# Moving the weights and the stationary tiles of a hybrid SSM and attention block to one SBUF address residue

## The chip, the cores and the metric

The kernel runs on one NeuronCore of one Trainium2 chip. The metric is the device time of one execution in microseconds (us), compared between kernels on the same chip. TensorE (PE) multiplies matrices: a weight load (PEld) puts the *stationary* operand into the array, and a matmul streams the *moving* operand past it. VectorE is DVE, ScalarE is ACT, GpSimd is POOL, and SyncE (SP) issues most DMAs. A tile of SBUF, the working memory, has 128 partitions, and its address is the byte at which it begins in each partition. "Residue" below is this address modulo 512.

## The reference

One layer over 2048 tokens of width 1024, all in float32:

```python
hn = rmsnorm(h, mix_norm_g[i])
proj = hn @ w_in[i]
u, g_ssm, q, k, v, g_attn = jnp.split(proj, SPLITS, axis=-1)
y_ssm = s5_branch(u, ...) * jax.nn.silu(g_ssm)           # diagonal complex SSM, GELU, GLU
y_att = stick_breaking_branch(q, k, v, q_norm_g[i], k_norm_g[i]) * jax.nn.silu(g_attn)
h = h + jnp.concatenate([y_ssm, y_att], axis=-1) @ w_out[i]
ple_gate = jax.nn.sigmoid(rmsnorm(h, ple_norm_g[i]) @ w_ple_gate[i])
h = h + ple_gate * (p[i] @ w_ple_proj[i])
```

The two 1024 x 1024 products at the end, with `w_out` and with `w_ple_gate`, are what the change is nearest to.

## The kernel before

**Split products.** A float32 product is made of three float32r products: each operand is split into a high part and the rest, and high x high, high x low and low x high are added up in PSUM. `mm3` (lines 541 to 543) does this with the weights as stationary operand, `mm3x` (lines 707 to 709) with the activations as stationary and 512 columns of weights as moving operand. `split` makes the parts: ACT copies the high part (line 513), DVE subtracts it (`vt`, line 65).

**Stages.** `phase_u` projects the SSM input (`ps_u`); SSM batches alternate with gate units (`ps_sg`) and the first attention projections (`ps_qk`); then come 40 steps of attention, in which four pairs of heads follow each other with a lag of 8 steps (projections `ps_q` on two halves of the rows, line 745; scores `ps_z`, line 812; transposes `ps_wt`, line 526; output `ps_o`, line 843). The GLU of the SSM branch (`ps_g2` and `ps_v2`, which the profile shows as `ps_g` and `ps_v` on `zr`) runs among the last ten steps.

**The output stage** is `phase_out`. For each of eight pairs of token tiles `mixed_pair` multiplies with `w_out` (`ps_h`), and then for each pair `gated_pair` multiplies with `w_ple_gate` (`ps_g` on `yr`) and with `w_pp` (`ps_p` on `pr`). Both use `cross_products`: a 2 x 2 block product with seven instead of eight block multiplications. For each of the seven, POOL or DVE forms a sum `sx` of blocks (line 912), `split` makes `yr` of it, and `mm3x` runs on four chunks of 128: 12 matmuls of 128 rows, 128 stationary and 512 moving columns. The weights of products 0 to 3 are in tiles `w` of the pool `w`, those of product 4 in halves of `xt` tiles (`wx`), those of products 5 and 6 in `wc` tiles of the pool `w3`. `gated_pair` first transposes `h` four times (`ps_t`, line 999).

In `mixed_pair` the callback `early` runs after product 2 and after product 3; `late` runs for each of the four output blocks and has ACT sum the squares of a block into a corner of `ss` (line 977).

**Where tiles lie.** Pools stand in two stacks: the left one grows up from byte 16512, the right one down from 229344. Within a pool the tags follow each other in the order of their first `tile()` call, and a slot takes a multiple of 32 bytes. At the bottom of the left stack is `const` (`warm` first, then `ident` and eight small tiles), above it `w` (16 weight tiles of 4096 bytes), `stage`, then `gx` and later `xp`, and at the end `fin`, which holds `yq`, `ss0`, `yr`, `sx`, `r`, `u` and small sums in this order. On the right are `kv0`, `proj`, `kv1`, `attn`, and at the end `w3` and `hr`, with `wc`, `wp`, `pr` and `h`. Keys and values are in `kv0`, `kv1` (right) and `kv2` (left), by the table `KV_SLOT`.

**Order.** `plan` collects what each instruction depends on, the bytes that a tile shares with older tiles included, `list_schedule` and `best_order` order every engine's instructions by estimated durations in six turns forward and back, and `arrange` writes that order down as dependences. An engine executes its own list in order; SP's list holds nearly all DMAs.

Of the kernel before, what the change touches and what calls it, by code (L numbers as in the profile page):

```python
# [8 lines left out]
F32 = mybir.dt.float32  # L9
# [3 lines left out]
AF = mybir.ActivationFunctionType  # L13
ALU = mybir.AluOpType
# [4 lines left out]
P = 128  # L19
# [44 lines left out]
def vt(nc, out, a, b, op):  # L64
    nc.vector.tensor_tensor(out, a, b, op=op)  # L65


def vs(nc, out, a, s1, op0, s2=None, op1=None):
    if op1 is None:
        nc.vector.tensor_scalar(out, a, s1, None, op0=op0)  # L70
    else:
        nc.vector.tensor_scalar(out, a, s1, s2, op0=op0, op1=op1)  # L72
# [830 lines left out]
def cross_products(e, pool, name, q, w, early, late, eng=None):  # L903

    nc = e.nc

    def f(tag, n):
        return pool.tile([P, 512], F32, tag=tag, name=tag, bufs=n)

    def add(a, b, op=ALU.add):  # L910
        t = f("sx", 3)
        (eng or nc.gpsimd).tensor_tensor(t, a, b, op=op)  # L912
        return t

    def product(ps, a, k, first):
        y = pool.tile([P, 2, 4, P], F32R, tag="yr", name="yr", bufs=4)
        split(e, y[:, 0].rearrange("p c t -> p (c t)"), y[:, 1].rearrange("p c t -> p (c t)"), a)
        for c in range(4):
            mm3x(e, ps, (y[:, 0, c], y[:, 1, c]), (w[k][c][:, 0], w[k][c][:, 1]), first and c == 0, c == 3, not first)

    ps = [e.bank(name, "z0", "z1", "acc", "ssm", "w0", *(("w1",) if name == "ps_h" else ())) for _ in range(4)]
    product(ps[0], q[0], 0, True)
    s1 = add(q[2], q[3])
    s2 = add(s1, q[0], ALU.subtract)
    r = f("r", 1)
    nc.scalar.activation(r, ps[0], AF.Copy)
    product(ps[1], s2, 1, True)
    u = f("u", 2)
    vt(nc, u, ps[1], r, ALU.add)
    product(ps[2], s1, 2, True)  # L930
    early(u, ps[2], 0)
    s3 = add(q[0], q[2], ALU.subtract)
    product(ps[3], s3, 3, True)
    early(u, ps[3], 1)
    product(ps[0], q[1], 4, False)
    late(0, ps[0], None)
    late(3, None, None)
    s4 = add(q[1], s2, ALU.subtract)
    product(ps[2], s4, 5, False)
    late(1, ps[2], u)  # L940
    product(ps[3], q[3], 6, False)
    late(2, ps[3], u)


def mixed_pair(e, pool, far, j):

    nc = e.nc
    dma = (nc.sync if j else nc.gpsimd).dma_start
    q, h = [], []
    for k in range(4):  # L950
        i = 2 * j + k // 2
        y = pool.tile([P, 512], F32, tag="yq", name="yq", bufs=5)
        v = y.rearrange("p (c t) -> p c t", c=4)
        if k % 2:
            dma(v, e.ya_d[i].rearrange("c p t -> p c t"))
        else:
            dma(v, e.ys_d[i // 4][:, (i % 4) * P:(i % 4 + 1) * P].rearrange("(c p) t -> p c t", p=P))
        q.append(y)
    for k in range(4):
        i = 2 * j + k // 2  # L960
        x = far.tile([P, 512], F32, tag="h", name="h", bufs=7)
        dma(x, e.x[0, i * P:(i + 1) * P, 512 * (k % 2):512 * (k % 2) + 512])
        h.append(x)
    ss = pool.tile([P, 2, 2], F32, tag=f"ss{j}", name="ss")

    def early(u, ps, n):
        if n == 0:
            for k in (3, 1, 2):
                nc.gpsimd.tensor_tensor(h[k], h[k], u, op=ALU.add)
        vt(nc, h[3], ps, h[3], ALU.add)  # L970

    def late(k, ps, u):
        if ps is not None:
            vt(nc, h[k], ps, h[k], ALU.add)
        i, m = k // 2, k % 2
        jk = far.tile([P, 512], F32, tag="sg", name="jk", bufs=4)
        nc.scalar.activation(jk, h[k], AF.Square, accum_out=ss[:, i, m:m + 1])
        nc.sync.dma_start(e.h_d[2 * j + i][:, 512 * m:512 * m + 512], h[k])

    cross_products(e, pool, "ps_h", q, e.wo, early, late, nc.vector if j < 2 else None)  # L980
    r = pool.tile([P, 2], F32, tag=f"rs{j}", name="rs")
    vt(nc, r, ss[:, :, 0], ss[:, :, 1], ALU.add)
    vs(nc, r, r, 1.0 / DM, ALU.mult, EPS, ALU.add)
    nc.gpsimd.tensor_tensor(r, r, e.mhalf[:, :2], op=ALU.pow)
    return r
# [51 lines left out]
def phase_out(e, pool, far, wpool2, wo4):  # L1037
    e.wo += [wo4] + [cross_weights(e, e.w_out[0], e.so_d, None, p, tag="wc", pool=wpool2, bufs=8) for p in range(5, 7)]
    rs = []
    for j in range(NT // 2):  # L1040
        rs.append(mixed_pair(e, pool, far, j))
        if j == 1:
            e.wp = [load_w(e, row_blocks(e.w_pp[0], 2, 512 * k), 512, None, tag="wp", pool=wpool2, bufs=4) for k in range(2)]
    e.wg = [cross_weights(e, e.w_pg[0], e.sg_d, e.gple, p, **(dict(pool=Halves(e)) if p == 4 else dict(tag="wc", pool=wpool2, bufs=8) if p > 4 else {})) for p in range(7)]
    for j in range(NT // 2):
        gated_pair(e, pool, far, j, rs[j])
# [3 lines left out]
def hybrid_block_kernel(ctx: ExitStack, tc: tile.TileContext, x, xt, small, p, w_in, ssm_w_glu, w_out, w_ple_gate,  # L1050
                        w_ple_proj, out, rows, pools, dbg=None):
    nc = tc.nc
# [25 lines left out]
    def const(name, shape, dt=F32):  # L1078
        return cp.tile(shape, dt, tag=name, name=name)

    warm = const("warm", [P, 1])
    nc.vector.memset(warm, 0.0)
    nc.scalar.activation(warm, warm, AF.Sigmoid)
    e.ident = const("ident", [P, P])
# [142 lines left out]
    for t in range(steps):  # L1227
# [7 lines left out]
        for hp in range(NHP):  # L1235
            i = t - SKEW * hp
# [385 lines left out]
```

## Time and profile before

| what | value |
|---|---|
| three runs | 1482.73, 1484.56, 1485.21 us; median 1484.56 us |
| span of the profiled execution, first to last instruction | 1479.9 us (the page gives that execution's time only as this span) |
| mean granted TensorE clock | 0.995 |
| PE busy | 1442.7 us, 97% of the span |
| weight loads busy, beside PE | 1222.7 us, 83% |
| DVE, ACT, POOL busy | 1010.3, 809.6, 473.1 us |
| DMA | 238.21 MB, mean 161 GB/s |

The runs' time also holds what lies before the first and after the last instruction. In the windows of the profile the columns are the stretch, its length, then busy time and number of instructions of each engine that has some (PE, PEld, DVE, ACT, POOL), the granted clock, the share of the DMA engines, and GB/s. In the timeline they are start and duration in us, engine, line, operation, out<-in (for a matmul, moving then stationary operand), and what the engine waited for. The duration of a matmul is modelled, and matmuls overlap; their starts are what can be compared. In the groups by tile the three numbers are the shortest, the median and the longest duration in ns.

### The profile page before, as it was taken

To read this page: it belongs to the slowest core of one execution; us is meant where nothing else is said; L and a number is where in the kernel's file an instruction comes from. 1 tells how busy PE (TensorE), PEld (TensorE's weight loads), DVE (VectorE), ACT (ScalarE), POOL (GpSimd) and SP (SyncE) were. 2 spreads that over 40 slices of the span, in tenths; PEclk is the share of its full clock that TensorE was granted. 3 is DMA by queue.
4 is the path that set the end of the run, shared out by engine and by line. 5 is a ranking of instruction groups with operands and counts; after the bars stand their busy time and mean duration, and the time that the engine had idled before them with its cause. 6 is when DMAs were issued, how large, how long until landed. Compare 5 with 4: busy or idle time off the path is not lost.

```text
span 1479.9 us, 33585 instructions
## 1 busy us (share of the span) xinstructions
PE 1442.7 (97%) x13068; PEld 1222.7 (83%) x13068; DVE 1010.3 (68%) x1817; ACT 809.6 (55%) x1765; POOL 473.1 (32%) x512
## 2 busy tenths in 40 slices
PE   6999999999999999999999999999999999999998
PEld 5999889988888888888888877787777887777776
DVE  8953877977567886678766766665787557844444
ACT  5654555655555766566655755465655435533332
POOL 3121364422221212121122115443234554433432
PEclk9999999999999999999999999999999999999999
DMA  8886846644333433334333455766477546423221
GB/s 289 286 285 208 247 140 192 198 155 154 136 134 114 149 116 115 107 123 143 116 129 126 125 133 188 237 204 185 137 245 244 182 156 209 143 71 100 86 74 55
DMA packets 179054, 238.21 MB, mean 161 GB/s; under 512 B 65760, under 2 KB 121296, under 8 KB 167760
## 3 DMA queue, kind: packets, MB, share of 16 engines
q1 hardware_dynamic: 176512, 227.49, 47.5%
q0 software_dynamic: 2384, 8.59, 2.0%
q8 instruction: 103, 1.69, 0.5%
q14 instruction: 55, 0.45, 0.1%
HBM read 166.94 MB, written 64.90 MB: 157 GB/s over the span
## 4 chain that ended last, share of the span: by engine, by line
PE 79%; DVE 9%; issue 3%; ACT 3%; POOL 3%; DMA 2%; SPq 0%; POOLq 0%; DVEq 0%; ACTq 0%
PE ps_q L745 21%; PE ps_o L843 8%; PE ps_z L812 6%; PE ps_wt L526 4%; PE ps_g L707 4%; PE ps_h L707 3%; PE ps_h L709 3%; PE ps_h L708 3%; PE ps_g L709 3%; PE ps_g L708 3%; DMA v<-qn 2%; PE ps_u L541 1%; PE ps_u L543 1%; PE ps_u L542 1%; POOL sx L912 1%
## 5 line engine op out<-in xcount | busy, mean ns | idle before, releaser
L821 DVE TENSOR_TENSOR_SCAN px<-px,ps_z 128x512 f32<-128x512 f32 (+3 forms) x320 | 339.9, 1085 | 84.8 <-ACT px L816 61.5
L745 PE MATMUL ps_q<-w_w,xt 64*128 64x512 f32 x2784 | 375.6, 398 | 1.3 <-DVE qn L65 0.7
L745 PEld LDWEIGHTS ps_q<-w_w,xt 64*128 64x128 f32 x2784 | 269.7, 185 | 39.9 <-DVE qn L65 2.0
L816 ACT ACTIVATE px<-ps_z 128x512 f32<-128x512 f32 (+3 forms) x320 | 159.2, 536 | 80.8 <-PE ps_z L812 79.5
L835 ACT ACTIVATE ws<-ps_wt 128x512 f32<-128x512 f32 (+3 forms) x320 | 160.8, 539 | 72.0 <-PE ps_wt L526 67.1
L812 PE MATMUL ps_z<-k,q 64*128 64x512 f32 (+3 forms) x960 | 137.8, 379 | 3.6 <-DVE px L821 1.8
L843 PE MATMUL ps_o<-ws,v 128*64 128x128 f32 x2176 | 135.2, 276 | 0.0
L843 PEld LDWEIGHTS ps_o<-ws,v 128*64 128x64 f32 x2176 | 117.6, 137 | 17.8 <-issue 14.9
L507 POOL TENSOR_TENSOR rs_qk<-rs_qk,mhalf 128x4 f32<-128x4 f32 x64 | 67.6, 1057 | 155.0 <-DVE rs_qk L72 152.4
L526 PEld LDWEIGHTS ps_wt<-ident,px 64*128 64x128 f32 x2176 | 95.5, 138 | 24.6 <-issue 5.5
L812 PEld LDWEIGHTS ps_z<-k,q 64*128 64x128 f32 x960 | 87.9, 186 | 21.6 <-issue 5.6
L526 PE MATMUL ps_wt<-ident,px 64*128 64x64 f32 x2176 | 101.0, 224 | 1.9 <-ACT ws L835 1.8
L819 POOL TENSOR_SCALAR_AFFINE_SELECT px<-px 128x128 f32<-128x128 f32 x128 | 40.6, 327 | 166.5 <-ACT px L816 157.3
L756 POOL TENSOR_TENSOR v<-qn,v 128x128 f32<-128x128 f32 x64 | 32.2, 504 | 161.4 <-DMA v<-qn 146.9
L541 PE MATMUL ps_u<-xt,w_w 128*128 128x256 f32 x256 | 75.5, 296 | 8.2 <-ACT w_w L491 6.9
L65 DVE TENSOR_TENSOR yr<-sx,yr 128x512 fp32r<-128x512 f32 x64 | 50.7, 814 | 42.0 <-ACT yr L513 41.2
L543 PE MATMUL ps_u<-xt,w_w 128*128 128x256 f32 x256 | 74.1, 296 | 2.0 <-DVE w_w L76 2.0
L542 PE MATMUL ps_u<-xt,w_w 128*128 128x256 f32 x256 | 74.9, 294 | 0.5 <-DVE xt L65 0.5
L1031 POOL TENSOR_TENSOR sg<-sg,h 128x512 f32<-128x512 f32 x28 | 39.6, 1414 | 95.6 <-DVE sg L65 94.2
L513 ACT ACTIVATE yr<-sx 128x512 fp32r<-128x512 f32 x64 | 39.1, 627 | 55.5 <-POOL sx L912 25.8
L65 DVE TENSOR_TENSOR qn<-ps_q,part 128x512 f32<-128x512 f32 x54 | 36.8, 681 | 42.7 <-ACT part L751 39.1
L513 ACT ACTIVATE yr<-yq 128x512 fp32r<-128x512 f32 x48 | 30.3, 631 | 55.4 <-PE ps_h L709 23.3
(438 smaller groups left out, 3492.3 us busy)
## 6 DMA issues: line engine op xcount, KB each, us to landing
xt<-hn SPq DMA_DIRECT2D x58, 1024.0 KB
hn<-xt SPq DMA_DIRECT2D x16, 1024.0 KB
h<-h SPq DMA_DIRECT2D x64, 256.0 KB
wst<-in_w_in_dram SPq DMA_DIRECT2D x48, 256.0 KB
xg<-hn SPq DMA_DIRECT2D x12, 1024.0 KB
out_dram<-sg SPq DMA_DIRECT2D x31, 256.0 KB
x<-in_x_dram SPq DMA_DIRECT2D x14, 512.0 KB
h<-in_x_dram SPq DMA_DIRECT2D x28, 256.0 KB
```

The source lines that it names most:

```text
L526: e.nc.tensor.transpose(ps[h][:, 64 * k:64 * k + 64], v[r], e.ident[r, r])
L541: mm(out, wh, xh, start=first, stop=False)
L542: mm(out, wh, xl, start=False, stop=False)
L543: mm(out, wl, xh, start=False, stop=last)
L707: mm(out, xh, wh, start=first, stop=False, skip_group_check=more)
L708: mm(out, xh, wl, start=False, stop=False, skip_group_check=more)
L745: nc.tensor.matmul(o, xt[r, a, c], A.w[c][r, b], start=c + s == 0, stop=c == NC8 - 1 and s == 2)
L812: nc.tensor.matmul(z[:, :n], q[half[h], a], A.k[ch][half[h], b, :n], start=s == 0, stop=s == 2)
L816: nc.scalar.activation(px[:, :n], z[:, :n], AF.Sigmoid, scale=-(HD ** -0.5))
L821: nc.vector.tensor_tensor_scan(rv, rv, z[:, :n][:, ::-1], initial=1.0 if carry[h] is None else carry[h], op0=ALU.mult, op1=ALU.bypass)
L835: nc.scalar.activation(dst, ps, AF.Copy, bias=1.0, scale=-1.0)
L843: nc.tensor.matmul(po[half[h], :P], A.v[sb][:, h], w[:, h, b], start=sb == i, stop=sb == 0)
```

## The change

Two allocations change; every instruction keeps its operands. The constant `warm`, of which one column is used, gets 24 columns. In `mixed_pair` the tile of the sums of squares, `ss`, is allocated when `early` first runs, after `yr`, `sx`, `r` and `u`, instead of at the start of the pair, between `yq` and `yr`. As each pair has its own tag `ss0` to `ss7`, only `ss0` stood before `yr`.

```diff
-    ss = pool.tile([P, 2, 2], F32, tag=f"ss{j}", name="ss")
+    sums = []
 
     def early(u, ps, n):
         if n == 0:
+            sums.append(pool.tile([P, 2, 2], F32, tag=f"ss{j}", name="ss"))
             for k in (3, 1, 2):
                 nc.gpsimd.tensor_tensor(h[k], h[k], u, op=ALU.add)
         vt(nc, h[3], ps, h[3], ALU.add)
...
-        nc.scalar.activation(jk, h[k], AF.Square, accum_out=ss[:, i, m:m + 1])
+        nc.scalar.activation(jk, h[k], AF.Square, accum_out=sums[0][:, i, m:m + 1])
...
-    vt(nc, r, ss[:, :, 0], ss[:, :, 1], ALU.add)
+    vt(nc, r, sums[0][:, :, 0], sums[0][:, :, 1], ALU.add)
...
-    warm = const("warm", [P, 1])
+    warm = const("warm", [P, 24])[:, :1]
```

## The prediction

> **What bounds the kernel now.** I read the page's first two parts, then the chain of work that ended last, then windows, waits and timeline of the last quarter, where the tiles lie that change their place against each other.
>
> ```profile
> span 1479.9 us, 33585 instructions
> PE 1442.7 (97%) x13068; PEld 1222.7 (83%) x13068; DVE 1010.3 (68%) x1817; ACT 809.6 (55%) x1765; POOL 473.1 (32%) x512
> PEclk9999999999999999999999999999999999999999
> PE 79%; DVE 9%; issue 3%; ACT 3%; POOL 3%; DMA 2%; SPq 0%; POOLq 0%; DVEq 0%; ACTq 0%
> ```
>
> TensorE is busy 97% of the span, at full clock, and holds 79% of the chain. An average says little about one stage, so here is the output stage (`ps_h` and `ps_g`, the only stage that reads `yr`), by windows and by PE's waits in it; the last window row counts the instructions on `yr` alone (PE, PEld, DVE, ACT).
>
> ```profile
> 1093.00:1253.00 160.00, 160.00 (x726) 128.25 (x723) 107.18 (x156) 75.70 (x157) 79.87 (x59) 1.00 0.64 206
> 1253.00:1281.00 28.00, 26.56 (x123) 20.76 (x122) 25.60 (x33) 18.65 (x34) 10.27 (x7) 1.00 0.58 185
> 1281.00:1475.00 194.00, 192.25 (x869) 151.98 (x867) 92.81 (x125) 71.49 (x119) 74.26 (x54) 1.00 0.25 80
> ...
> PE ps_g L707 <- ACT yr L513: 2.7, 6, 1.2
> PE ps_t L999 <- ACT yq L1001: 0.2, 1, 0.2
> ...
> 1093.00:1475.00 382.00, 325.28 (x1344) 248.50 (x1344) 96.83 (x112) 67.96 (x111) 1.00 0.44 141
> ```
>
> PE is busy 378.8 of these 382 us and waits 2.9 us in all: a matmul that takes less is time off the end. 1344 matmuls use `yr` as stationary operand. The mean duration of a matmul is modelled and pipelined, so I take the distance between starts. One unbroken run of `ps_h`, first and last row, with its window row (541 matmuls):
>
> ```profile
> 1125.44 0.40 PE L707 MATMUL ps_h<-w_w,yr 128*128 128x512 f32 x1
> ...
> 1251.44 0.39 PE L709 MATMUL ps_h<-w_wc,yr 128*128 128x512 f32 x1
> ...
> 1125.44:1251.44 126.00, 126.00 (x541) 101.25 (x540) 38.72 (x45) 26.44 (x42) 1.00 0.58 188
> ```
>
> 126.00 us over 540 steps is **233.3 ns** a matmul. Now the same form of matmul (128 rows, 128 columns, 512 moving columns, three per block as in the split product) on other tiles: `ps_p` inside this stage, `ps_v` of the GLU, `ps_qk` of the first projections.
>
> ```profile
> 1369.51 0.39 PE L707 MATMUL ps_p<-w_wp,pr 128*128 128x512 f32 x1
> ...
> 1372.25 0.27 PE L999 MATMUL ps_t<-ident,h 128*128 128x128 f32 x1
> ...
> 1079.05 0.39 PE L541 MATMUL ps_v<-zr,w_w 128*128 128x512 f32 x1
> ...
> 1081.55 0.39 PE L543 MATMUL ps_v<-zr,w_w 128*128 128x512 f32 x1
> ...
> 195.51 0.40 PE L708 MATMUL ps_qk<-w_w,xg 128*128 128x512 f32 x1
> ...
> 200.51 0.39 PE L709 MATMUL ps_qk<-w_w,xg 128*128 128x512 f32 x1
> ...
> 1341.85 0.39 PE L707 MATMUL ps_p<-w_wp,pr 128*128 128x512 f32 x1
> ...
> 1344.39 0.39 PE L709 MATMUL ps_p<-w_wp,pr 128*128 128x512 f32 x1
> ```
>
> Twelve `ps_p` take 2.74 us (228.3 ns each); `ps_v` takes 2.50 us for 11 steps (227.3), `ps_qk` 5.00 us for 22 (227.3); the slowest unbroken run of `ps_p`, the last two rows, takes 2.54 us for 11 (230.9). So a `yr` product costs some 5 ns more than these, in the same stage too.
>
> **The change part by part.** First the addresses. The left pools start at 16512, a slot takes a multiple of 32 bytes: `warm` 32, `ident` 512 and eight small constants of 32 put the weights at 17312, which is 416 modulo 512. All that follows up to `fin` is a multiple of 512, so `w`, `xg`, `xt`, `zr` are all at 416. In `fin` come five `yq` (10240 bytes), then `ss0` (32 bytes), so `yr` starts at **448**. The right pools go down from 229344 (480): `wc`, `wp`, `pr` are at 480. So today `ps_qk`, `ps_v` (416 with 416) and `ps_p` (480 with 480) have both operands at one residue, and only the `yr` products do not: 448 with 416 (five of seven products of a pair) or with 480 (two).
>
> *`warm` of 24 columns.* Its slot grows from 32 to 96 bytes, so every left tile moves up by 64: weights, `xt`, `zr` to 480. The instructions on it still take one column: cost 0, with nothing needed to hide it.
>
> *`ss` allocated in `early`.* No instruction or DMA is issued by an allocation, none passes another queue. Its slot now follows `yr`, `sx`, `r`, `u`, so `yr` moves by 64 - 32: 448 to 480, the residue of `w`, `wx`, `wc`. `sums[0]` is made before its first use in `late`; no wait is added.
>
> *The price of a `yr` matmul afterwards.* No `yr` product at equal residues is in this trace, so I bound it by the rows above: 227.3 at best, 230.9 at worst; 228.0 is taken, nearest to `ps_p` of the same stage, which has the same neighbours. Could the 5 ns come from other engines' traffic instead? This stretch has DVE, ACT and POOL all idle (window row, then first and last matmul on `yr` in it):
>
> ```profile
> 1305.70:1308.10 2.40, 2.40 (x12) 1.94 (x11) 0.00 (x0) 0.00 (x0) 0.00 (x0) 1.00 0.50 155
> ...
> 1305.62 0.40 PE L709 MATMUL ps_g<-w_wc,yr 128*128 128x512 f32 x1
> ...
> 1307.72 0.40 PE L709 MATMUL ps_g<-w_wc,yr 128*128 128x512 f32 x1
> ```
>
> Nine steps in 2.10 us: 233.3 with nothing else running. Traffic isn't it, nor the moving operand, since `w_w` at 416 and `w_wc` at 480 give the same. What is left to tell the groups apart is where `yr` lies. PEld is busy 101.25 of the 126.00 us in which PE streams, so both operands are read at once, and a clash that depends on their addresses is possible. 1344 x (233.3 - 228.0) = **7.1 us**; with the bounds 3.2 us (230.9) to 8.1 us (227.3).
>
> The Trainium skill speaks against this: the page "SBUF — State Buffer", section "Who interferes with whom", gives TensorE two independent read ports, one for the moving operand and one for weight loads, and says that it never waits on anyone. By that rule a residue costs nothing, and the sum would be 0. The rows above differ by 5 ns where only the address is known to differ, so the sum goes by them.
>
> *What is given back.* In a gated pair one chain beside PE nearly ends last:
>
> ```profile
> 1369.05 0.60 ACT L1001 ACTIVATE yq<-ps_t 128x512 f32<-128x512 f32 x1 [0.85 <-PE ps_t L999]
> ...
> 1369.79 1.28 POOL L912 TENSOR_TENSOR sx<-yq 128x512 f32<-128x512 f32 x1 [1.69 <-ACT yq L1001]
> ...
> 1371.15 1.29 POOL L912 TENSOR_TENSOR sx<-sx,yq 128x512 f32<-128x512 f32 x1
> ...
> 1372.48 1.15 ACT L513 ACTIVATE yr<-sx 128x512 fp32r<-128x512 f32 x2 [2.17 <-POOL sx L912]
> ...
> 1373.16 0.50 PE L707 MATMUL ps_g<-w_w,yr 128*128 128x512 f32 x1 [0.32 <-ACT yr L513]
> ```
>
> It starts at the pair's fourth transpose and is already 0.32 us late at product 1. Only three `yr` matmuls lie behind that transpose (the rest are `ps_p`), so 3 x 5.3 ns x 8 pairs = 0.1 us is lost there; everything earlier on PE also starts the chain earlier.
>
> *The other tiles that move.* Transposes take one price whatever the residue of their stationary operand (`h` 480, `bn` 128, `lt` 384; median in the middle), so `ident` going from 160 to 224 costs 0:
>
> ```profile
> L999 PE MATMUL ps_t<-ident,h x128: 270/272/331, 1251.7 to 1450.9; 128*128 128x128 f32 x128
> L340 PE MATMUL ps_pack<-ident,bn x64: 270/272/301, 126.0 to 280.4; 128*128 128x128 f32 x64
> L352 PE MATMUL ps_pack<-ident,lt x16: 270/272/328, 136.3 to 286.5; 128*128 128x128 f32 x16
> ```
>
> The keys in left-hand slots 2, 5, 6, 7 go from 416 to 480, the residue of `q`. They serve 56 of the 160 block-chunk steps, three row pairs each: 168 pairs, bounded by 5.3 ns either way, is 0.9 us; I take 0, since keys lie at 480, 384 and 416 today. ACT's writes of `yr` cost the same as its writes of tiles already at 480:
>
> ```profile
> L513 ACT ACTIVATE yr<-sx 128x512 fp32r<-128x512 f32 x64 | 39.1, 627 | 55.5 <-POOL sx L912 25.8 <-PE ps_h L709 15.9 <-PE ps_g L709 13.3
> L513 ACT ACTIVATE w_wc<-wst 128x512 fp32r<-128x512 f32 x12 | 7.1, 622 | 1.8 <-DMA wst<-in_w_out_dram 1.6
> L513 ACT ACTIVATE pr<-pt 128x512 fp32r<-128x512 f32 x8 | 5.0, 628 | 0.0
> ```
>
> **Sum:** 7.1 - 0.1 = 7.0 us off the profiled execution's 1479.9 us. The median of the runs, 1484.56 us, stands 4.7 us above that span, for what lies around it, and no part of the change touches that: 1484.56 - 7.0 = **1477.6 us**.
>
> **The rivals.**
>
> *Residue means nothing, or `yr` doesn't land at 480* (had `ss0` kept its place, `yr` would be at 0 against 480, 32 apart as today). Then 1484.6 us. For it: no run in this trace has `yr` anywhere else, so the 5 ns could belong to something about `yr` that I don't see, such as being freshly written. The skill's rule above would end here. Against it: `pr`, written in the same way in the same stage, doesn't pay it.
>
> *The feed becomes the bound in the gated half.* If faster products only lengthen PE's wait for `yr`, half of the 1344 count: 672 x 5.3 = 3.6 us, so 1481.0 us. For it: the 0.32 us wait in every pair. Against it: that wait covers one product of seven, and DVE is busy 92.81 of 194 us.
>
> *Slower: the written order shifts at the hand-over to the output stage.* The planner takes dependences from addresses. Today `yr`'s first slot reaches 32 bytes into the old key buffer of slot 6; afterwards it ends where that begins, and its second slot no longer reaches slot 7. Two waits fall away and none comes, but ranks of the last GLU unit's load and store on the SP queue can change, and with them the order there. The price is one load that comes late for PE; the longest such piece in the chain is this:
>
> ```profile
> 692.11 9.68 DMA v<-qn
> ```
>
> One of that size turns -7.0 into +2.7: 1487.3 us; it decides from 7.0 us of new PE wait on. Against it: the yr writers have later predecessors than the lost ones (`cross_sums`' stores use slot 5, which `yr` still covers), so the order of the start isn't set by what falls away.
>
> **How the numbers follow.** Forecast 0.76; no effect 0.12; half 0.07; slower order 0.05. The forecast's own range is 8.1 + 0.9 to 3.2 us of gain and about 1.2 us of spread of the median (the three runs lie 2.5 us apart): 1474.4 to 1482.6. That also holds the half case, so 1474.4 to 1482.8 has some 0.8 of the chance. 0.2% (3.0 us) is about what a measurement of this kernel tells from no change: the forecast and most of the half case are beyond it, so faster 0.79, the same 0.15, slower 0.06.
>
> **What would show it.** Starts in a long `ps_h` run 228 ns apart instead of 233.3; the output stage some 7 us shorter, about evenly in `ps_h` and `ps_g`; `ps_p`, `ps_v`, `ps_qk` and the transposes as before, and the first `ps_h` still near 1093 us. Wrong: `yr` steps still at 233 (no effect); 228 in both halves but PE waiting for `yr` for more than 6 us (feed); a first `ps_h` later than 1095 us (order).

## The result, and the profile after

| | before | after |
|---|---|---|
| median of five runs | 1483.95 us | 1477.46 us |
| lowest and highest run | 1481.51 to 1485.21 us | 1474.24 to 1477.69 us |
| ratio, 95% interval | | 0.9955 [0.9943, 0.9967] |
| span of the profiled execution | 1479.9 us | 1472.5 us |

The change makes the kernel 0.45% faster (0.33 to 0.57%), about 6.5 us; 7.0 us were forecast. First the page of the changed kernel: its span, the busy time of the engines, the granted clock, the chain of work that ended last.

```profile
span 1472.5 us, 33586 instructions
PE 1436.7 (98%) x13068; PEld 1224.2 (83%) x13068; DVE 1009.0 (69%) x1817; ACT 810.4 (55%) x1765; POOL 474.8 (32%) x512
PEclk8999999999999999999999999999999999999999
PE 81%; DVE 7%; DMA 3%; ACT 3%; issue 3%; POOL 2%; SPq 1%; POOLq 0%; DVEq 0%; ACTq 0%
```

PE has the same 13068 matmuls and is busy 6.0 us less; weight loads are busy 1.5 us more (1224.2 instead of 1222.7 us). Now the output stage: three windows that follow the three of before (`ps_h`; the first gated pair; the rest), PE's only waits in it, and the window row of the instructions on `yr` alone.

```profile
1093.00:1249.75 156.75, 156.73 (x728) 128.31 (x724) 108.78 (x157) 76.06 (x159) 79.50 (x59) 1.00 0.64 209
1249.75:1277.00 27.25, 26.04 (x124) 20.77 (x123) 24.34 (x32) 18.44 (x34) 10.95 (x7) 1.00 0.58 190
1277.00:1468.00 191.00, 189.10 (x868) 151.70 (x866) 92.76 (x124) 71.39 (x119) 74.16 (x54) 1.00 0.26 82
...
PE ps_g L707 <- ACT yr L513: 2.8, 6, 1.2
...
1093.00:1468.00 375.00, 318.09 (x1344) 248.35 (x1344) 97.76 (x112) 67.83 (x111) 1.00 0.44 143
```

The stage is over at 1468 instead of 1475 us. The 1344 instructions on `yr` keep PE busy 318.09 us instead of 325.28. PE waits for `yr` as often as before, 2.8 us in all. The step between starts, from the timeline: first and last row of the longest unbroken `ps_h` run, with its window row.

```profile
1130.55 0.39 PE L708 MATMUL ps_h<-w_wc,yr 128*128 128x512 f32 x1
...
1235.29 0.39 PE L707 MATMUL ps_h<-w_w,yr 128*128 128x512 f32 x1
...
1130.55:1235.29 104.74, 104.74 (x464) 86.71 (x462) 62.00 (x89) 46.69 (x98) 60.42 (x44) 1.00 0.55 181
```

462 steps in 104.74 us are **226.7 ns**; it was 233.3. Over every step between two `yr` matmuls in which PE didn't stop (under 260 ns; some 1240 steps) the mean is 227.4 instead of 233.3. Of the products whose operands keep their place against each other, `ps_v` and the transposes are where they were: in the last run of `ps_v` 11 steps take 2.49 us (2.50 before), and the middle duration of a transpose stays at 272 ns. `L1000` is line 999 of before.

```profile
1079.11 0.39 PE L541 MATMUL ps_v<-zr,w_w 128*128 128x512 f32 x1
...
1081.60 0.39 PE L543 MATMUL ps_v<-zr,w_w 128*128 128x512 f32 x1
...
L1000 PE MATMUL ps_t<-ident,h x128: 270/272/330, 1248.0 to 1443.8; 128*128 128x128 f32 x128
L340 PE MATMUL ps_pack<-ident,bn x64: 270/272/300, 125.6 to 280.1; 128*128 128x128 f32 x64
```

`ps_p` gets faster too, although both its operands lay at 480 before and after: over its steps under 260 ns the mean falls from 228.6 to 227.6 ns. One of its runs of six matmuls, first and last row, in the kernel before and then in the changed kernel:

```profile
1387.45 0.40 PE L707 MATMUL ps_p<-w_wp,pr 128*128 128x512 f32 x1
...
1388.61 0.39 PE L709 MATMUL ps_p<-w_wp,pr 128*128 128x512 f32 x1
```

```profile
1381.45 0.39 PE L707 MATMUL ps_p<-w_wp,pr 128*128 128x512 f32 x1
...
1382.58 0.39 PE L709 MATMUL ps_p<-w_wp,pr 128*128 128x512 f32 x1
```

Five steps take 1.16 us before and 1.13 us after. Both runs stand right behind a `yr` product; why that matters is taken up at the end.

**The length of the stage** is the sharper measure. From the start of the first `ps_h` to the start of the last `ps_p` the kernel before takes 381.90 us and the changed one 374.42: **7.48 us**. Both begin near 1093.1 us, but a second profile of the changed kernel began at 1096.7 us:

```profile
L707 PE MATMUL ps_h<-w_w,yr x128: 387/389/498, 1096.7 to 1246.8; 128*128 128x512 f32 x128
...
L709 PE MATMUL ps_p<-w_wp,pr x64: 388/389/477, 1254.5 to 1471.2; 128*128 128x512 f32 x64
```

Same kernel, 3.6 us later, most of it gathered in a few places of the attention; its stage takes 374.47 us. So executions differ by some 4 us ahead of this stage, while in these two profiles the stage repeats to 0.05 us. Below, each experiment is read by its steps and its stage, and by its time only where repeated executions give an interval.

### The profile page after: what moved, and what is told of

Its sections match the earlier page's. It is cut to its first block, busy times and chain, and to the rows that moved or that the text cites. A ratio compares the mean times of both kernels' runs of the same rounds, so it can differ in the third digit from the quotient of the medians.

```text
span 1472.5 us, 33586 instructions
## 1 busy us (share of the span) xinstructions
PE 1436.7 (98%) x13068; PEld 1224.2 (83%) x13068; DVE 1009.0 (69%) x1817; ACT 810.4 (55%) x1765; POOL 474.8 (32%) x512
## 4 chain that ended last, share of the span: by engine, by line
PE 81%; DVE 7%; DMA 3%; ACT 3%; issue 3%; POOL 2%; SPq 1%; POOLq 0%; DVEq 0%; ACTq 0%
PE ps_q L745 21%; PE ps_o L843 7%; PE ps_z L812 6%; PE ps_wt L526 4%; PE ps_g L707 4%; PE ps_h L709 4%; PE ps_h L707 3%; PE ps_h L708 3%; PE ps_g L709 3%; PE ps_g L708 3%; DMA v<-qn 2%; PE ps_u L541 1%; PE ps_u L543 1%; PE ps_u L542 1%; PE ps_sg L541 1%
```

## The experiments

**Theory A**, the prediction's: a 512-column float32r matmul takes less when its operands lie at one residue. **Rival B**: the residue means nothing; it is something else about the change, such as the place of `ss`. **Rival C**: it is `yr`'s own place, whatever the weights do. After the first results the question became which distance counts, and modulo what. "Distance" is address of `yr` minus address of the weights.

### Half of the change: `warm` alone

The kernel before with only the first edit, so `w`, `wx`, `wc` at 480 and `yr` at 0, still 32 apart:

```diff
-    warm = const("warm", [P, 1])
+    warm = const("warm", [P, 24])[:, :1]
```

> Only the first half of the change: warm gets 24 columns, ss keeps its place. Every left-hand tile is 64 bytes higher than before, weights at residue 480, but yr is at 0, so the yr products stay 32 bytes apart (0 against 480). All engines' lists are those of before. Theory 'equal residues of stationary and moving operand': yr steps stay at 233.3 ns and the time at 1484 us, within 0.2% of before. Rival 'the shift of the other left-hand tiles (keys, identity, SSM tiles) is what helped': the whole gain of 6.5 us shows here, 1477.5 us, with the yr steps at any price.

Measured: 1484.18 us, ratio 0.9996 [0.9986, 1.0006]. First and last row of its longest `ps_h` run:

```profile
1129.92 0.39 PE L707 MATMUL ps_h<-w_w,yr 128*128 128x512 f32 x1
...
1255.92 0.39 PE L709 MATMUL ps_h<-w_wc,yr 128*128 128x512 f32 x1
```

540 steps in 126.00 us: 233.3, and a stage of 381.89 us, as before. Moving the weights to the place that they have in the changed kernel does nothing by itself.

### The other half: `ss` alone

The changed kernel without the wider `warm`: `w`, `wx` and `yr` at 416, `wc` at 480, 64 away.

```diff
-    warm = const("warm", [P, 24])[:, :1]
+    warm = const("warm", [P, 1])
```

> Only the second half: ss is allocated in early, warm keeps one column. yr is at 416, where w and wx are, and wc stays at 480, 64 bytes apart. The engines' lists are those of the change. Theory 'residues must be equal modulo 512': products 0 to 4 run at 226.7 ns a step, products 5 and 6 (on wc) stay at 233.3, gain 5/7 of 6.5, so about 1479.3 us. Theory 'only the residue modulo 64 counts': all seven products at 226.7, 1477.5 us. Rival 'the written order, not the address, brought the gain': 1477.5 us with steps that do not depend on the weights' tile.

Measured: 1478.02 us, ratio 0.9951 [0.9936, 0.9966]. One run on `wc`, then one on `w` and `wx`:

```profile
1151.15 0.40 PE L707 MATMUL ps_h<-w_wc,yr 128*128 128x512 f32 x1
...
1156.43 0.39 PE L709 MATMUL ps_h<-w_wc,yr 128*128 128x512 f32 x1
...
1175.82 0.40 PE L707 MATMUL ps_h<-w_w,yr 128*128 128x512 f32 x1
...
1189.24 0.39 PE L709 MATMUL ps_h<-wx,yr 128*128 128x512 f32 x1
```

On `w` and `wx` 59 steps in 13.42 us are 227.5, on `wc` 23 in 5.28 us are 229.6. The stage takes 375.81 us, 1.39 more than the changed kernel's. So equal residues at 416 do as well as at 480, which speaks for A and against `yr`'s own place. But the step on `wc`, between the 226.7 and the 233.3 that two readings of A gave, fits neither: the distance has a size.

### Residue 448 for all but `wc`

If the residue 448, where `yr` lay before, were bad in itself, its steps would stay at 233.

```diff
-    warm = const("warm", [P, 24])[:, :1]
+    warm = const("warm", [P, 16])[:, :1]
```

> The change with warm at 16 columns: weights w at 448, wx at 448 and yr at 448, wc still at 480. All engines' lists are those of the change. Theory 'what counts is the distance between the two operands': yr steps on w and wx at 227 ns, on wc (32 apart) at 233.3, time about 1479.5 us (960 x 6.4 ns less than before, less some 0.7 us given back). Rival 'residue 448 itself is slow for yr, which is why before was slow': all yr steps at 233.3, 1484.6 us.

Measured: 1479.5 us, ratio 0.9977 [0.9964, 0.9990]. The steps on `w` are 228.2 in the mean and 227 at the most frequent, on `wx` 226.7, and on `wc`, 32 away:

```profile
1151.46 0.40 PE L707 MATMUL ps_h<-w_wc,yr 128*128 128x512 f32 x1
...
1156.83 0.40 PE L709 MATMUL ps_h<-w_wc,yr 128*128 128x512 f32 x1
```

23 steps in 5.37 us: 233.5. The stage takes 377.00 us, 2.58 more than the changed kernel's; 384 matmuls on `wc` x (233.4 - 226.8, their mean in the changed kernel) = 2.5 us. With the first run this rules out B and C: the same residue of `yr` gives 227 or 233 within one stage, by the weights that it meets.

### The same `yr`, other weights moved away

Only `w` is moved, 32 bytes below all else, by an untouched 32-byte tile behind it.

```diff
-    warm = const("warm", [P, 24])[:, :1]
+    warm = const("warm", [P, 16])[:, :1]
...
     e.stage = [pool(ctx, "stage", STB)] * STB
+    e.stage[0].tile([P, 8], F32, tag="gap", name="gap", bufs=1)
```

> The change with the pool of weights alone moved back by 32 bytes: w at 448, and yr, wx, wc, xt, xg, zr at 480 as in the change. It takes the equality away from products that had it before too. Theory 'distance between the two operands, whatever the tile': yr steps on w rise from 227 to 233.3, on wx and wc stay at 227; the GLU's steps (ps_v on zr) and ps_qk rise from 227 to 233. Then 768 + 480 matmuls pay 6.4 ns again: 8.0 us more than the change, 1485.5 us, if the matmuls of 256 columns (ps_u, ps_sg) and the row pairs (ps_q) pay nothing; up to 1503 us if those 1536 and 1440 pairs pay 6 ns each as well. Rival 'it is something about yr': ps_v and ps_qk stay at 227, and the time is at most 1482.5 us.

Measured: 1483.7 us, ratio 1.0004 [0.9992, 1.0016]: the whole gain is gone. A run on `w` and, further on, one on `wc`:

```profile
1157.92 0.40 PE L707 MATMUL ps_h<-w_w,yr 128*128 128x512 f32 x1
...
1168.89 0.40 PE L709 MATMUL ps_h<-w_w,yr 128*128 128x512 f32 x1
...
1171.87 0.39 PE L707 MATMUL ps_h<-w_wc,yr 128*128 128x512 f32 x1
...
1177.09 0.39 PE L709 MATMUL ps_h<-w_wc,yr 128*128 128x512 f32 x1
```

47 steps in 10.97 us (233.4) against 23 in 5.22 us (227.0), with `yr` unmoved. The stage takes 378.27 us, so about half of the stage's gain (3.85 of 7.48 us) is lost in it. The other readers of `w`, ahead of it, pay too: unbroken products of `ps_v` go from 226.6 to some 233.4, `ps_qk` from 228.4 to 233.2, the row pairs of `ps_q` from 230 to 233 in the median. The expected loss was larger all the same, since one group went the other way: the 256-column `ps_u` and `ps_sg` fell from 120 to 117 ns. That is taken up last.

### The size of the distance

Three kernels, in each of which four `yr` tiles take turns, at four distances from weights that all lie at 480. Columns added to a tile move the ones behind it. The first of the three:

```diff
-        y = pool.tile([P, 2, 4, P], F32R, tag="yr", name="yr", bufs=4)
+        n = e.turn = getattr(e, "turn", -1) + 1
+        name, size, at = (("yra", 1040, 0), ("yrb", 1040, 0), ("yrc", 1048, 0), ("yrd", 1024, 0))[n % 4]
+        y = pool.tile([P, size], F32R, tag=name, name=name)[:, at:at + 1024].rearrange("p (s c t) -> p s c t", s=2, c=4)
```

> The change, with the four buffers of yr as four tiles yra, yrb, yrc, yrd at 0, 64, 128 and 256 bytes from the residue of the weights (480). Each product uses the next one. Theory 'equal modulo 512': yra 226.7 ns a step, the other three 233.3. Theory 'equal modulo 64': all four 226.7. A clash that depends on the distance in some other way shows as different steps of yrb, yrc and yrd; if one of them is below 226.7, there is a better place than the equal one. Time 1477 us (modulo 64) or 1483 us (modulo 512); the planner's order differs from that of before and of the change, so only the steps count here.

> As the kernel with four places, but yra, yrb, yrc and yrd at 16, 32, 96 and 192 bytes from the residue of the weights. Theory 'equal modulo 64': only yrd (192) at 226.7 ns a step, yrb and yrc at 233.3, yra (16) at 233.3 too or between. Theory 'equal modulo 512': all four at 233.3. Theory 'equal modulo 32' falls by the kernel before (32 apart, 233.3).

> As the kernels with four places of yr, with yra, yrb, yrc, yrd at 160, 224, 384 and 448 bytes from the residue of the weights. So far 0 gives 227 ns a step, 256 gives 228.7, 192 and 448 give 230, 16 gives 231, and 32, 64, 96, 128 give 233 to 234. If the distance repeats after 256 bytes: yra (160) unknown, yrb (224) at 233.3 as 480 in the kernel before, yrc (384) as 128, 232.7, yrd (448) as 192, 230. If it repeats after 512 only, yrc may lie anywhere between 227 and 234.

Measured: 1478.93, 1482.29 and 1480.85 us, one execution each; the new tags change the order of some instructions, so only the steps are compared. Mean step within a product, over all products on the tile (the range is over `w`, `wx` and `wc`):

| distance, bytes | ns | distance, bytes | ns |
|---|---|---|---|
| 0 | 227.2 to 228.0 | 256 | 228.5 to 229.6 |
| 16 | 229.7 to 232.0 | | |
| 32 | 232.8 to 233.2 | | |
| 64 | 233.4 to 233.5 | | |
| 96 | 233.7 to 234.4 | | |
| 128 | 232.6 to 233.1 | 384 | 232.5 to 233.1 |
| 160 | 233.3 to 233.8 | | |
| 192 | 229.5 to 231.1 | 448 | 229.4 to 229.9 |
| 224 | 233.3 to 233.4 | | |

One product (12 matmuls, 11 steps) at 64 and one at 256, from the timeline of the first kernel:

```profile
1302.70 0.40 PE L707 MATMUL ps_g<-w_wc,yrb 128*128 128x512 f32 x1
...
1305.27 0.39 PE L709 MATMUL ps_g<-w_wc,yrb 128*128 128x512 f32 x1
...
1357.96 0.39 PE L707 MATMUL ps_g<-w_wc,yrd 128*128 128x512 f32 x1
...
1360.45 0.39 PE L709 MATMUL ps_g<-w_wc,yrd 128*128 128x512 f32 x1
```

2.57 us against 2.49: some 233.5 and 226.6 ns. The means that stand side by side in the table agree at 128 and 384 and at 192 and 448. At 256 the mean is 1 to 2 ns above that at 0; in most of its products on `ps_h` this lies in the first three steps behind a product at 128 (229, 232, 231 ns), and then the steps are 226 to 227 as at 0. The order of single steps shows the same: at 192 and at 448 they go round 226, 229, 232 ns, at 128 and at 384 alike mostly round 230, 232, 241, 232, 231, 232, 228 ns. So the pattern repeats after **256** bytes, not 512; a pattern of 64 bytes is excluded by 64 itself. Equal addresses are the best place, and 192 is about half way, which is what `wc` paid with `ss` moved alone (416 - 480 is 192 modulo 256).

The means hide something. In the second kernel a product at distance 16 takes one of two prices:

```profile
1236.28 0.40 PE L707 MATMUL ps_h<-w_wc,yra 128*128 128x512 f32 x1
...
1238.85 0.39 PE L709 MATMUL ps_h<-w_wc,yra 128*128 128x512 f32 x1
...
1301.36 0.39 PE L707 MATMUL ps_g<-w_wc,yra 128*128 128x512 f32 x1
...
1303.85 0.39 PE L709 MATMUL ps_g<-w_wc,yra 128*128 128x512 f32 x1
```

2.57 and 2.49 us, same tile, same kind of weights. In the first row the product ahead has a `yr` at 192, in the second it is a `ps_p` at 0. So at some distances the step also depends on something beside the operands' distance. The tile of the product ahead doesn't decide it alone: behind a `yr` at 192 most whole products at 16 take some 233.5, but two take 226.6.

### Which operand waits

The high part of `yr` stays at 0, the low part (`yl`) goes 32 bytes away; each chunk runs high, high, low (lines 707, 708, 709).

```diff
-        y = pool.tile([P, 2, 4, P], F32R, tag="yr", name="yr", bufs=4)
+        y = [pool.tile([P, 4, P], F32R, tag="yr", name="yr", bufs=4)]
+        if not hasattr(e, "gap"):
+            e.gap = pool.tile([P, 8], F32, tag="gap", name="gap", bufs=1)
+        y.append(pool.tile([P, 4, P], F32R, tag="yl", name="yl", bufs=4))
```

> The changed kernel with the high and the low part of the stationary operand in tiles of their own: the high part yr at 0 from the weights, the low part yl 32 bytes away. Each chunk then runs yr on the high weights (line 707), yr on the low weights (708), yl on the high weights (709). Theory N (the moving stream meets the load of the next stationary operand): the step that begins at 708 takes 233.3 ns, those from 707 and 709 take 227, so three matmuls 687 ns. Theory O (it meets the operand already in the array, so the step of the matmul itself counts): the step from 709 takes 233.3, those from 707 and 708 227. Theory M (what counts is the pair of weight loads that follow each other): 708 and 709 both lie above 227, 707 doesn't. Time about 1480 us, since a third of the yr steps lose 6.6 ns, 3 us.

Measured: 1484.65 us in one execution (its order differs too). First and last row of its longest run:

```profile
1128.37 0.39 PE L707 MATMUL ps_h<-w_w,yr 128*128 128x512 f32 x1
...
1231.93 0.40 PE L707 MATMUL ps_h<-w_wc,yr 128*128 128x512 f32 x1
```

444 steps in 103.56 us: 233.2, the full price, with only every third stationary operand moved. By line, the mean step within a product is 231.8 ns from 707, 237.7 from 708, 229.0 from 709. The largest lies where the load of the moved operand runs beside the stream of the matmul ahead, which is the place of theory N, but the sum is 698.5 ns and not N's 687, and the step between two unmoved operands is above 227 as well. None of the three theories holds as it was put. That the load of the next operand is what meets the moving stream fits the largest step; it isn't shown.

### All moving streams at one address

The transposes' identity and the keys of the remaining slots are brought to 480 as well.

```diff
-    e.ident = const("ident", [P, P])
-    make_identity(nc, e.ident)
...
+    held = {n: const(n, [P, k]) for n, k in (("gmix", NC8), ("gple", NC8), ("bglu", NC8), ("gq", 1), ("gk", 1))}
+    e.ident = const("ident", [P, P])
+    make_identity(nc, e.ident)
...
-    r = pool.tile([P, n], F32, tag=f"rs_{tag}", name=f"rs_{tag}")
+    r = pool.tile([P, 112 if tag == "qk" else n], F32, tag=f"rs_{tag}", name=f"rs_{tag}")[:, :n]
```

> The change, and also the identity (224), the keys and values of the right-hand pool kv1 (384), px and ws (384) moved to residue 480, so that transposes, scores and attention outputs have both operands at 480 too (slots 0 and 2, 5, 6, 7 of the keys and values had it in the change already, apart from ws). Theory 'only float32r matmuls of 128 rows clash': steps of ps_wt, ps_o, ps_t, ps_z and the time are as with the change, 1477.5 us, ratio to it within 0.2%. Rival 'any two operands apart cost': 2176 transposes ps_wt and 2176 ps_o at 1 to 3 ns less each give 4 to 13 us less, 1465 to 1473 us.

Measured: 1476.99 us, ratio 0.9954 [0.9941, 0.9968], the same as the change. The pairs of transposes `ps_wt` (62 ns), four steps of `ps_o` (218 ns) and the 128-column products of the SSM keep their prices. The scores on keys at 480 take 227 at the lower quartile of a row pair instead of 231 to 232. So of the forms tried, the ones that clearly pay for a distance are float32r streams of 512 columns; length and type were not varied one at a time. Moving these tiles brings nothing more.

### A better version? `xg` and `xt` away from `w`

As the 256-column products got faster with `w` moved away, the version that takes both gains keeps the changed kernel and moves only their other operand, by 32 and by 128 bytes; the changed kernel runs once more beside them.

```diff
-    e.row = [gx.tile([P, 256], F32, tag=f"row{T}", name=f"row{T}") for T in range(1)]
+    e.row = [gx.tile([P, 264], F32, tag=f"row{T}", name=f"row{T}")[:, :256] for T in range(1)]
```

> The changed kernel with the table of the gates' rotation 32 bytes longer, so that xg and the SSM input xt lie 32 bytes away from the weights, and everything from the attention on as in the changed kernel. Theory A (256-column matmuls go the other way, as in the kernel with w moved away, where their median step fell from 120 to 117 ns): 1536 matmuls of ps_u and ps_sg step at 117, which takes 4 us off PE's work, of which some 2 us show, since part of it turns into wait for weights; ps_qk (96 matmuls) goes from 228 to 233, 0.6 us lost. First ps_h about 1 to 2 us earlier, time 1475 to 1477 us. Theory B (the faster 256-column steps came from w's own place): steps stay at 120, ps_qk at 233, time 1478 us.

> As the kernel before this, but 128 bytes instead of 32. Theory A with the curve of the 512-column matmuls turned round: ps_u and ps_sg between 117 and 118, ps_qk near 232.7, time 1475 to 1477 us. Theory B: steps stay at 120, ps_qk at 232.7, 1478 us.

> The changed kernel once more, on the same chip as these two: the ratio to the kernel before as first measured, 0.9955, 256-column steps at 120, yr steps at 226.7 to 228.

| | median, us | ratio to before | 256-column step, median | `ps_qk` step, mean | stage, us |
|---|---|---|---|---|---|
| the change again | 1477.11 | 0.9960 [0.9947, 0.9972] | 120 | 227.8 | 374.47 |
| 32 apart | 1475.43 | 0.9955 [0.9942, 0.9967] | 117 | 233.3 | 374.45 |
| 128 apart | 1476.35 | 0.9964 [0.9950, 0.9977] | 119 | 232.7 | 374.48 |

One run of 53 `ps_sg` matmuls in the changed kernel, and the same run 32 apart:

```profile
167.52 0.36 PE L541 MATMUL ps_sg<-xg,w_w 128*128 128x256 f32 x1
...
173.83 0.28 PE L542 MATMUL ps_sg<-xg,w_w 128*128 128x256 f32 x1
```

```profile
166.77 0.36 PE L541 MATMUL ps_sg<-xg,w_w 128*128 128x256 f32 x1
...
172.92 0.28 PE L542 MATMUL ps_sg<-xg,w_w 128*128 128x256 f32 x1
```

6.31 us against 6.15: the opposite sign is real in the steps. In the time it can't be told from nothing; the three intervals overlap. Against the first profile of the changed kernel, the gate units are 0.9 us ahead at 298 us, and at the last `ps_sg` (313.48 against 313.66 us) 0.2 us, since PE has waited 0.9 us for DVE in between. Against its second profile, whose last `ps_sg` is at 314.66 us, the lead there is still 1.2 us; yet the first `ps_h` comes at 1097.1 us, after that profile's 1096.7. So a lead of this size is lost in the differences between executions that the attention makes.

## Why the prediction was right

- **PE bounds the output stage.** Right: it is busy 371.87 of the 375.00 us, and the stage shrank by about what the `yr` matmuls saved.
- **The 5 ns belong to where `yr` lies against its weights.** Right, and now tried from both sides: `yr` moved with the weights fixed, the weights moved with `yr` fixed. The page "SBUF — State Buffer" of the Trainium skill, section "Who interferes with whom", by which the two read ports of TensorE are independent and it waits on nobody, doesn't agree with 226.7 against 233.3 ns; the measurement decides.
- **Price of 228.0 ns.** Mis-sized: the mean is 227.4, close to the prediction's better bound of 227.3, and long runs go at 226.7. The term is 1344 x 5.9 = 7.9 us instead of 7.1. The 228.0 leaned on `ps_p`, which was itself slowed by the `yr` products next to it. Nor is 230.9 its slowest run: runs of six matmuls take up to 231.2, one of five 232.0.
- **0.1 us given back at product 1.** Mis-sized: 7.9 less the stage's 7.48 is 0.4 us, and more by what `ps_p` gained. In the gated pairs product 1 is as late as it was (0.34 us, row below, 0.32 before), as foretold. What was missed is `ps_h`, which had one unbroken run of 541: six of its steps were over 300 ns before, 0.57 us too long in all, and nine are afterwards, 1.0 us in all. At one of the places the load waits for DVE, and the step behind it, 0.31 us, is 0.08 too long (the last three rows).

```profile
1394.66 0.50 PE L707 MATMUL ps_g<-w_w,yr 128*128 128x512 f32 x1 [0.34 <-ACT yr L513]
...
1130.21 0.19 PEld L707 LDWEIGHTS ps_h<-w_wc,yr 128*128 128x128 f32 x1 [0.25 <-DVE h L65]
...
1130.24 0.47 PE L707 MATMUL ps_h<-w_wc,yr 128*128 128x512 f32 x1
1130.55 0.39 PE L708 MATMUL ps_h<-w_wc,yr 128*128 128x512 f32 x1
```

- **The time, 1477.6 us against 1477.46 measured.** That it is so close is luck. The gain is about 6.5 us against 7.0, but the sum starts from 1484.56 us, the median of three runs, and the median of five is 1483.95; and the two mis-sized terms partly cancel, 0.8 us too little saved and some 0.3 us too little given back.
- **Other moved tiles at 0.** Right for the transposes. The keys that came to `q`'s residue gain some 3 ns in the median of a row pair (234 to 231), on 168 pairs 0.5 us, inside the bound of 0.9. That this comes from their address isn't shown: the keys of slot 0, which stay at 480, fall from 232.7 to 230.0 ns in the mean as well.
- **4.7 us around the span.** Wrong in its naming: the changed kernel's profiled run took 1474.24 us with a span of 1472.5, so 1.7 us lie around it. If as much lay around the span of before, the rest of the 4.7 is that the execution that was profiled was one of the shorter ones. The forecast didn't lean on it, as it is a difference.
- **The sign that a first `ps_h` later than 1095 us means a new order** was no good sign: the kernel with `warm` alone began at 1097.5 us, and the changed kernel itself at 1096.7 in its second profile, with each engine's order unchanged.

The rivals: *no effect* falls with the two halves of the change. *The feed becomes the bound in the gated half* falls: `ps_g` got 3.49 us shorter, `ps_h` 3.72 (first to last start of each), where the rival had nothing for `ps_g`. *The written order shifts* falls: the instructions of DVE, ACT, POOL and SP come in the same order as before, and PE's too but for a few neighbours of 64 rows that start within 0.25 us of each other.

## What to carry to other kernels

When PE sets the end, compare the start-to-start step of matmuls of one form across tiles: a group that is a few per cent slower at full clock, also where the other engines are idle, may differ only in the distance between its operands. Here 512-column float32r products wanted both operands at the same address modulo 256, and a small padding did it; it is worth trying on whichever form holds most of the time, as the 256-column form preferred the opposite. Judge such a change by the length of the stage, which repeated to 0.05 us here in two profiles while whole executions differed by 4 us.

## What the hardware showed that was not expected

- The price of a distance has a period of 256 bytes and isn't a simple step: 227 at 0, 233 to 234 from 32 to 160, 230 at 192, 233 again at 224.
- The price belongs to a stream more than to a single matmul. At distance 16 the same product takes 226.6 or 233.5 ns, and one moved operand of three costs as much as all three (233.2). What sets the rhythm stays open.
- Equal addresses don't give 226.7 at once. In the changed kernel 11 of 88 whole `yr` products take over 228 ns a step, and each of them stands right behind a step of over 300 ns. In the rows below such a step comes first; then five steps take 1.16 us, the next five 1.13 us. The single steps behind it are 231, 236, 228, 233, 231 and then 226 to 227 ns. In the kernel before, the slow runs of `ps_p` go through the same kind of steps (236, 224, 231, 236, 228 ns) behind a `yr` product, without a stop. So at equal addresses the stream settles within some ten steps, and a short product behind a stop or behind a product at another distance pays on the way there.

```profile
1341.45 0.50 PE L709 MATMUL ps_g<-w_w,yr 128*128 128x512 f32 x1
1341.79 0.39 PE L707 MATMUL ps_g<-w_w,yr 128*128 128x512 f32 x1
...
1342.95 0.39 PE L709 MATMUL ps_g<-w_w,yr 128*128 128x512 f32 x1
...
1344.08 0.39 PE L707 MATMUL ps_g<-w_w,yr 128*128 128x512 f32 x1
```

- 256-column products go the other way: 120 ns at distance 0, 117 at 32, 119 at 128. Why is open as well.
